# Places of matmul operands in SBUF: odd and even multiples of 64 bytes for the weight buffers and the FFN inputs of a two-layer decoder trunk

## Chip, core and metric

The kernel runs on one core of one Trainium2 chip. The metric is the device time of one launch in microseconds; lower is better. Before the change the median of three runs is 2210.63 us (2208.31 to 2213.5).

## What is computed

A decoder trunk of two layers works on x of 512 tokens by 1024 features, all in float32. Cut to what matters:

```python
def swiglu(h, w_gate, w_up, w_down):
    return (jax.nn.silu(h @ w_gate) * (h @ w_up)) @ w_down

for i in range(DEPTH):                       # DEPTH = 2
    x = x + 0.5 * swiglu(rmsnorm(x, g[0]), ...)   # D_FF = 2816
    h = rmsnorm(x, g[1])
    x = x + (attn_mixer(h, ...) if i % 2 == 0 else mamba2_mixer(h, ...))
    x = x + 0.5 * swiglu(rmsnorm(x, g[2]), ...)
return rmsnorm(x, final_norm)
```

So there are four FFNs (`swiglu`), one attention mixer and one state-space mixer (SSM), in the order FFN 0, attention, FFN 1, FFN 2, SSM, FFN 3.

## The kernel before

Everything is kept transposed: features on the 128 partitions, tokens along the free dimension. Every float32 product is made of three TensorE matmuls on a split of both operands, `a = ah + al`: `mm3` (lines 121 to 125) issues weights `whi` with moving `xh` (line 123), `whi` with `xl` (line 124) and `wlo` with `xh` (line 125). Each matmul loads its own 128 x 128 weights first, so in the profile each PE MATMUL has a PEld LDWEIGHTS with the same operands. The program gives the moving operand as the last input of a matmul and the weights as the first; the profile prints the moving operand first (`bs<-xh,whi`: output `bs`, moving `xh`, weights `whi`).

- **Weights.** A weight tile comes from HBM into `raw` (two buffers, SyncE's queue). `split` (line 92) makes `whi` by a rounding copy on ScalarE (line 98) and `wlo` by a subtraction on VectorE (line 99). `split_dma` (line 104) makes `whi` and a negated copy on ScalarE (lines 110, 111) and adds `raw` by a DMA of GpSimd's queue (line 112). `whi` and `wlo` have three buffers each, used in turn, in one pool (line 46). Each buffer is 4096 bytes in a partition. `values` (line 373) takes its value weights from the same buffers.
- **FFN inputs.** `open_x` (line 144) opens a pool at the upper end of SBUF before each stage. For an FFN `xh` and `xl` are 32768 bytes each: for every one of 4 feature blocks 8 pieces of 256 tokens, seven of which are the operands of a Strassen scheme, so that a gate and up block takes 7 products instead of 8. For the attention and the SSM they are 16384 bytes each and a filler tile of 64 bytes follows (line 158). `edge` (line 50) takes the last 32 bytes.
- **One FFN** (`ffn`, line 1096) has two halves. In each, 11 calls of `gate_up` (line 1176) make 7 products x 4 feature blocks x 3 = 84 matmuls of 256 columns each (output `bs`), and then the down projection makes 8 x 11 x 3 = 264 matmuls of 512 columns (output `bm`, moving `ah`, `al`). The first block of each FFN (the first two of FFN 0) has no Strassen scheme: `gate_up_direct` (line 1139), 2 x 8 x 3 = 48 matmuls of 512 columns. The last output tile of FFN 3 is made in two halves of 256 columns by `last` (line 1263).
- **The rest.** The projections of the attention and the SSM are `mm3` of 512 columns with moving `xh`, `xl`, the output projections have moving `qh`, `ql` and `yh`, `yl`.

The order of the instructions on each engine is set by a scheduler when the program is built, with time estimates of its own; the tile pools give each tile its place in SBUF, from the lower end or from the upper end (`side="right"`). The places of the built program, in bytes from the start of a partition: `whi` 33664, 37760, 41856, `wlo` 45952, 50048, 54144, `ah` 78720, `al` 101248; `xh` 163776 and `xl` 196544 in all four FFNs; `xh` 196480 and `xl` 212864 in the attention and the SSM. Divided by 64 the FFNs' `xh` and `xl` give odd numbers, all the others even ones. Every slice that a matmul of these tiles takes starts a multiple of 128 bytes into its tile, except half of those of `values`, so the tile's place tells odd or even.

Of the kernel before, what the change touches and what calls it, by code (L numbers as in the profile page):

```python
# [14 lines left out]
F32 = mybir.dt.float32  # L15
F32R = mybir.dt.float32r
# [5 lines left out]
P = 128  # L22
# [7 lines left out]
FFN_NORMS = (0, 2, 3, 5)  # L30
# [10 lines left out]
class Trunk:  # L41
    def __init__(self, ctx, tc, aps):
        self.ctx, self.tc, self.nc, self.aps = ctx, tc, tc.nc, aps
        nc = self.nc
        self.cst = ctx.enter_context(tc.tile_pool(name="cst", bufs=1))
        self.wp = ctx.enter_context(tc.tile_pool(name="wp", bufs=3))
        self.rawp = ctx.enter_context(tc.tile_pool(name="rawp", bufs=2))
        self.one = ctx.enter_context(tc.tile_pool(name="one", bufs=1))

        edge = ctx.enter_context(tc.tile_pool(name="edge", bufs=1, side="right"))  # L50
        edge.tile([P, 8], F32, name="edge")
        self.xT = self.cst.tile([P, ND, T], F32, name="xT")
        self.xpool = None
        self.gains = self.cst.tile([P, 7, ND], F32, name="gains")
        nc.sync.dma_start(out=self.gains, in_=aps["gains"])
        self.epsc = self.cst.tile([P, 1], F32, name="epsc")
        nc.vector.memset(self.epsc, EPS)
        self.onesD = self.cst.tile([P, P], F32, name="onesD")
        nc.vector.memset(self.onesD, 1.0 / D)
        self.n = 0  # L60
        self.ahead = None
        nc.scalar.preload_act_table_set("natural_log_exp_and_others")
# [25 lines left out]
    def row(self, tag):  # L88
        self.n += 1
        return self.one.tile([P, T], F32, tag=tag, name=f"{tag}_{self.n}")  # L90

    def split(self, raw, n, lo_engine=None):

        nc = self.nc
        self.n += 1
        hi = self.wp.tile([P, 8, P], F32R, tag="whi", name=f"whi_{self.n}")
        lo = self.wp.tile([P, 8, P], F32R, tag="wlo", name=f"wlo_{self.n}")
        nc.scalar.copy(out=hi[:, :n], in_=raw)  # L98
        (lo_engine or nc.vector).tensor_tensor(  # L99
            out=lo[:, :n], in0=raw, in1=hi[:, :n].bitcast(F32), op=ALU.subtract  # L100
        )
        return hi, lo

    def split_dma(self, raw, n):

        nc = self.nc
        self.n += 1
        hi = self.wp.tile([P, 8, P], F32R, tag="whi", name=f"whi_{self.n}")
        lo = self.wp.tile([P, 8, P], F32R, tag="wlo", name=f"wlo_{self.n}")
        nc.scalar.copy(out=hi[:, :n], in_=raw)  # L110
        nc.scalar.activation(out=lo[:, :n], in_=raw, func=AF.Copy, scale=-1.0)  # L111
        nc.gpsimd.dma_start(out=lo[:, :n], in_=raw, accum_op=ALU.add)  # L112
        return hi, lo
# [30 lines left out]
    def open_x(self):  # L144

        self.close_x()
        self.r = None
        if self.which == 6:
            return
        self.n += 1  # L150
        self.strassen = self.which in FFN_NORMS
        self.xpool = self.tc.tile_pool(name=f"x{self.n}", bufs=1, side="right", reuse_waits="tile")
        pool = self.xpool.__enter__()
        shape = [P, 4, 8, 256] if self.strassen else [P, ND, T]
        self.xh = pool.tile(shape, F32R, name=f"xh_{self.n}")
        self.xl = pool.tile(shape, F32R, name=f"xl_{self.n}")
        if not self.strassen:
            pool.tile([P, 16], F32, name=f"xe_{self.n}")

    def close_x(self):  # L160
# [212 lines left out]
    def values(self, rc):  # L373

        nc, aps, A = self.nc, self.aps, self.A
        gate = A.tile([P, NB, 24], F32, name="gate")
        banks = [self.bank(t) for t in "ttom"]
        for c in range(4):
            raw = self.load(aps["wv"][:, 2 * c : 2 * c + 2], [P, 2, 408])
            self.n += 1  # L380
            hi = self.wp.tile([P, 2, 408], F32R, tag="whi", name=f"whi_{self.n}")
            lo = self.wp.tile([P, 2, 408], F32R, tag="wlo", name=f"wlo_{self.n}")
            nc.scalar.copy(out=hi, in_=raw)
            nc.gpsimd.tensor_tensor(out=lo, in0=raw, in1=hi.bitcast(F32), op=ALU.subtract)
            for j in range(2):
                k = 2 * c + j
                for t in range(NB):
                    ts = slice(t * P, t * P + P)
                    self.mm3(
                        banks[t][:, 0:408], self.xh[:, k, ts], self.xl[:, k, ts], hi[:, j], lo[:, j], k == 0, k == ND - 1  # L390
                    )
        for t in range(NB):
            b = banks[t]
            src = b[:, 0:384].rearrange("p (a g d) -> p a g d", a=3, g=2)
            dst = [v[:, t].rearrange("p a (h d) -> p a h d", h=3)[:, :, 0:3:2] for v in (self.vh, self.vl)]
            nc.scalar.activation(out=dst[0], in_=src, func=AF.Copy, scale=rc[:, t : t + 1])
            for g in range(2):
                nc.vector.scalar_tensor_tensor(
                    out=dst[1][:, :, g],
                    in0=src[:, :, g],  # L400
                    scalar=rc[:, t : t + 1],
                    in1=dst[0][:, :, g].bitcast(F32),
                    op0=ALU.mult,
                    op1=ALU.subtract,
                )
            nc.vector.tensor_scalar(
                out=gate[:, t], in0=b[:, 384:408], scalar1=rc[:, t : t + 1], scalar2=None, op0=ALU.mult
            )
        nc.scalar.activation(out=gate, in_=gate, func=AF.Exp, scale=-1.0)
        nc.vector.tensor_scalar(out=gate, in0=gate, scalar1=1.0, scalar2=None, op0=ALU.add)  # L410
        nc.vector.reciprocal(out=gate, in_=gate)
        self.gate = gate.rearrange("p t (g j r) -> p t g j r", g=2, j=4)
# [985 lines left out]
```

## Time and profile before

| | |
|---|---|
| median of three runs | 2210.63 us (2208.31 to 2213.5) |
| the profiled execution | 2213.22 us, of which the span of its instructions is 2211.4 us |
| PE (matmul) busy | 2139.6 us, 97% of the span, 13488 matmuls |
| PEld (weight loads) busy | 1919.7 us, 87% |
| VectorE, ScalarE, GpSimd busy | 75%, 52%, 36% |
| granted TensorE clock, mean | 0.987 of full speed |
| chain that ended last | PE 85%, VectorE 8%, ScalarE 3%, issue 2%, DMA 2% |

The profiled execution is one launch on the chip. The time of a launch is the span plus what lies around it, here 2213.22 - 2211.4 = 1.8 us. A matmul's end in the profile is modelled (matmuls overlap in the array), so its duration tells little; the time from one matmul's start to the next one's start is what a stream of them costs. The chain is followed back from the last instruction, at each step to what released it.

### The profile page before, as it was taken

Reading aid. Unit: us, or ns where it says so; the run is one execution under the profiler, and the core shown is the slowest. Engines: PE = TensorE matmul, PEld = TensorE weight load, DVE = VectorE, ACT = ScalarE, POOL = GpSimd, SP = SyncE. Lnnn points to the kernel's source line nnn. Section 1 sums busy time; section 2 is a strip of 40 time slices with the busy share of each in tenths; the row PEclk is TensorE's granted clock in tenths of the full one; section 3 lists DMA queues with packets and bytes.
Section 4 is the critical chain, followed back from the end, with each engine's and each line's share of the span. In section 5 each row is a group of like instructions: output and inputs, shape, how many; then the busy total and the mean of one; then the engine's idle time right before and its main releaser. Section 6 shows DMA issues by size and latency. Waiting matters only on the chain.

```text
span 2211.4 us, 34462 instructions
## 1 busy us (share of the span) xinstructions
PE 2139.6 (97%) x13488; PEld 1919.7 (87%) x13488; DVE 1659.7 (75%) x2495; ACT 1157.1 (52%) x1813; POOL 805.4 (36%) x602
## 2 busy tenths in 40 slices
PE   8999999988999999999999999999999998999997
PEld 6999997877887998998998997788888877998996
DVE  6966975586788976987985985677667668975974
ACT  7533544455566533545542544677667666543543
POOL 1613621532013623622632630244444435623630
PEclk9999999979999999999999999999999999999999
DMA  3222325416302322322332324656565652232332
GB/s 134 96 100 102 115 99 155 128 49 154 77 1 67 115 98 103 108 102 94 109 104 97 115 93 127 153 144 152 125 155 144 162 143 61 102 106 101 109 104 78
DMA packets 48450, 242.05 MB, mean 109 GB/s; under 512 B 6624, under 2 KB 9696, under 8 KB 31136
## 3 DMA queue, kind: packets, MB, share of 16 engines
q1 hardware_dynamic: 36048, 195.28, 25.7%
q0 software_dynamic: 12240, 44.57, 10.7%
q8 instruction: 106, 1.74, 0.3%
q14 instruction: 56, 0.46, 0.1%
HBM read 193.04 MB, written 2.23 MB: 88 GB/s over the span
## 4 chain that ended last, share of the span: by engine, by line
PE 85%; DVE 8%; ACT 3%; issue 2%; DMA 2%; POOL 0%; SPq 0%; DVEq 0%; ACTq 0%; POOLq 0%
PE bm L123 13%; PE bm L125 13%; PE bm L124 13%; PE bs L123 13%; PE bs L125 12%; PE bs L124 12%; DMA wlo<-raw 1%; PE bt L541 1%; DVE wlo L99 1%; DVE xl L249 1%; PE bs L492 1%; PE bo L556 1%; PE bs L487 1%; PE bo L553 1%; PE bs L493 0%
## 5 line engine op out<-in xcount | busy, mean ns | idle before, releaser
L123 PE MATMUL bs<-xh,whi 128*128 128x256 f32 (+1 forms) x2404 | 680.0, 286 | 7.6 <-ACT xh L248 3.6
L124 PE MATMUL bs<-xl,whi 128*128 128x256 f32 (+1 forms) x2404 | 679.8, 285 | 5.7 <-DVE xl L249 5.7
L125 PE MATMUL bs<-xh,wlo 128*128 128x256 f32 (+1 forms) x2404 | 669.2, 285 | 2.0 <-DVE wlo L99 1.9
L98 ACT CAST whi<-raw 128x1024 fp32r<-128x1024 f32 (+3 forms) x312 | 257.0, 827 | 403.5 <-PE bm L124 188.1
L123 PEld LDWEIGHTS bs<-xh,whi 128*128 128x128 f32 x2404 | 452.1, 188 | 17.6 <-ACT whi L98 5.8
L124 PEld LDWEIGHTS bs<-xl,whi 128*128 128x128 f32 x2404 | 452.0, 188 | 12.6 <-DVE xl L249 7.6
L125 PEld LDWEIGHTS bs<-xh,wlo 128*128 128x128 f32 x2404 | 446.7, 188 | 7.9 <-DVE wlo L99 2.8
L99 DVE TENSOR_TENSOR wlo<-raw,whi 128x1024 fp32r<-128x1024 f32 (+3 forms) x304 | 332.2, 1093 | 91.3 <-ACT whi L98 89.8
L1173 POOL TENSOR_TENSOR sa<-raw 128x512 f32<-128x512 f32 x82 | 113.2, 1381 | 654.7 <-DMA raw<-wgu 297.8
L125 PE MATMUL bm<-ah,wlo 128*128 128x512 f32 (+1 forms) x715 | 275.9, 386 | 0.0
L124 PE MATMUL bm<-al,whi 128*128 128x512 f32 (+1 forms) x715 | 275.8, 386 | 0.0
L123 PE MATMUL bm<-ah,whi 128*128 128x512 f32 (+1 forms) x715 | 274.8, 386 | 0.0
L112 POOL DMA_DIRECT2D wlo<-raw x85 | 73.7, 867 | 449.5 <-ACT wlo L111 443.9
L123 PE MATMUL bm<-xh,whi 128*128 128x512 f32 x488 | 194.2, 398 | 5.8 <-DVE t L858 3.5
L125 PE MATMUL bm<-xh,wlo 128*128 128x512 f32 x488 | 192.8, 395 | 4.2 <-DMA wlo<-raw 4.1
L124 PE MATMUL bm<-xl,whi 128*128 128x512 f32 x488 | 192.4, 395 | 0.0
L1173 POOL TENSOR_TENSOR sa<-sa,raw 128x512 f32<-128x512 f32 x82 | 166.6, 2031 | 5.6
L125 PEld LDWEIGHTS bm<-ah,wlo 128*128 128x128 f32 x715 | 134.3, 188 | 27.2
L124 PEld LDWEIGHTS bm<-al,whi 128*128 128x128 f32 x715 | 134.3, 188 | 26.8
L123 PEld LDWEIGHTS bm<-ah,whi 128*128 128x128 f32 x715 | 134.3, 188 | 26.8
L99 DVE TENSOR_TENSOR wlo<-sb,whi 128x1024 fp32r<-128x1024 f32 x83 | 150.8, 1817 | 0.0
L1218 DVE TENSOR_TENSOR gu<-gu,bs 128x512 f32<-128x512 f32 (+1 forms) x249 | 147.4, 592 | 2.7
(400 smaller groups left out, 4168.9 us busy)
## 6 DMA issues: line engine op xcount, KB each, us to landing
raw<-wgu SPq DMA_DIRECT2D x88, 1024.0 KB
raw<-wdn SPq DMA_DIRECT2D x64, 704.0 KB
wlo<-raw POOLq DMA_DIRECT2D x85, 512.0 KB, 4.7
raw<-m_win SPq DMA_DIRECT2D x24, 1024.0 KB
raw<-m_wout SPq DMA_DIRECT2D x8, 1024.0 KB
raw<-wqk SPq DMA_DIRECT2D x6, 1024.0 KB
raw<-cw SPq DMA_DIRECT2D x4, 1024.0 KB
raw<-wo SPq DMA_DIRECT2D x4, 1024.0 KB
```

The source lines that it names most:

```text
L98: nc.scalar.copy(out=hi[:, :n], in_=raw)
L99: (lo_engine or nc.vector).tensor_tensor(out=lo[:, :n], in0=raw, in1=hi[:, :n].bitcast(F32), op=ALU.subtract)
L112: nc.gpsimd.dma_start(out=lo[:, :n], in_=raw, accum_op=ALU.add)
L123: nc.tensor.matmul(out, wh, xh, start=start, stop=False)
L124: nc.tensor.matmul(out, wh, xl, start=False, stop=False)
L125: nc.tensor.matmul(out, wl, xh, start=False, stop=stop)
L249: nc.vector.tensor_tensor(out=lo, in0=src, in1=hi.bitcast(F32), op=ALU.subtract)
L487: nc.tensor.matmul(s[j], q_hi, k_hi, start=True, stop=False)
L492: nc.tensor.matmul(s[j], q_hi, k_lo, start=False, stop=False)
L541: nc.tensor.transpose(t[:, at : at + P], p[:, j, k0 : k0 + P], self.idf)
L1173: engine.tensor_tensor(out=out, in0=x, in1=y, op=op)
L1218: nc.vector.tensor_tensor(out=out, in0=x, in1=y, op=ALU.add)
```

## The change

It changes where tiles stand in SBUF and nothing else. The instructions, their order on each engine and their semaphore waits are the same in both built programs.

```diff
-        self.wp = ctx.enter_context(tc.tile_pool(name="wp", bufs=3))
+        self.wph = ctx.enter_context(tc.tile_pool(name="wph", bufs=3))
+        apart = ctx.enter_context(tc.tile_pool(name="apart", bufs=1))
+        apart.tile([P, 16], F32, name="apart")
+        self.wpl = ctx.enter_context(tc.tile_pool(name="wpl", bufs=3))
+        apart2 = ctx.enter_context(tc.tile_pool(name="apart2", bufs=1))
+        apart2.tile([P, 16], F32, name="apart2")
...
+    def weight_tiles(self):
+        tiles = (
+            pool.tile([P, 8 * P + 16], F32R, tag=tag, name=f"{tag}_{self.n}")
+            for pool, tag in ((self.wph, "whi"), (self.wpl, "wlo"))
+        )
+        return [t[:, : 8 * P].rearrange("p (k m) -> p k m", m=P) for t in tiles]
...
-        hi = self.wp.tile([P, 8, P], F32R, tag="whi", name=f"whi_{self.n}")
-        lo = self.wp.tile([P, 8, P], F32R, tag="wlo", name=f"wlo_{self.n}")
+        hi, lo = self.weight_tiles()
...
+        form = FFN_NORMS.index(self.which) if self.strassen else 1
         self.xh = pool.tile(shape, F32R, name=f"xh_{self.n}")
+        if form > 1:
+            pool.tile([P, 16], F32, name=f"xm_{self.n}")
         self.xl = pool.tile(shape, F32R, name=f"xl_{self.n}")
-        if not self.strassen:
+        if form in (1, 2):
             pool.tile([P, 16], F32, name=f"xe_{self.n}")
```

`split` and `split_dma` take their tiles from `weight_tiles`, `values` from `wph` and `wpl`. A weight buffer grows by 64 bytes, so the middle one of the three stands at an odd multiple of 64. The places after the change:

| tile | before | after |
|---|---|---|
| `whi`, three buffers | 33664 even, 37760 even, 41856 even | 33664 even, 37824 odd, 41984 even |
| `wlo`, three buffers | 45952 even, 50048 even, 54144 even | 46208 even, 50368 odd, 54528 even |
| `xh`, `xl` of FFN 0 | 163776 odd, 196544 odd | 163776 odd, 196544 odd |
| `xh`, `xl` of FFN 1 | 163776 odd, 196544 odd | 163712 even, 196480 even |
| `xh`, `xl` of FFN 2 | 163776 odd, 196544 odd | 163648 odd, 196480 even |
| `xh`, `xl` of FFN 3 | 163776 odd, 196544 odd | 163712 even, 196544 odd |
| `xh`, `xl` of attention, SSM | 196480 even, 212864 even | the same |
| `ah`, `al` | 78720 even, 101248 even | 79232 even, 101760 even |

The other tiles from the lower end stand 512 bytes higher, and so keep odd or even.

## Rows read from the trace of the kernel before

**Rows 1.** The page: busy time of the engines (us, share of span, instructions), then the chain.

```profile
PE 2139.6 (97%) x13488; PEld 1919.7 (87%) x13488; DVE 1659.7 (75%) x2495; ACT 1157.1 (52%) x1813; POOL 805.4 (36%) x602
...
PE 85%; DVE 8%; ACT 3%; issue 2%; DMA 2%; POOL 0%; SPq 0%; DVEq 0%; ACTq 0%; POOLq 0%
```

**Rows 2.** Groups by line and shape: count, busy us, mean ns, idle before, releasers.

```profile
L123 PE MATMUL bs<-xh,whi 128*128 128x256 f32 x2324 | 647.3, 281 | 2.6 <-ACT whi L98 1.1 <-DVE al L249 0.7 <-DVE gu L1218 0.3
...
L123 PE MATMUL bm<-ah,whi 128*128 128x512 f32 x693 | 268.4, 389 | 0.0
L123 PE MATMUL bm<-xh,whi 128*128 128x512 f32 x488 | 194.2, 398 | 5.8 <-DVE t L858 3.5 <-DVE xT L1234 1.6 <-DVE z L858 0.7
...
L123 PE MATMUL bm<-yh,whi 128*128 128x512 f32 x128 | 51.0, 402 | 0.0
...
L123 PE MATMUL bm<-qh,whi 128*128 128x512 f32 x64 | 26.4, 412 | 0.7 <-ACT qh L248 0.7
```

**Rows 3.** Busy us (instructions) of PE by stretch, granted clock, DMA share, GB/s.

```profile
196.20:304.90 108.70, 108.70 (x925) 1.00 0.29 101
136.40:196.10 59.70, 59.70 (x265) 1.00 0.31 108
2189.35:2194.60 5.25, 5.25 (x46) 1.00 0.00 0
1030.90:1041.80 10.90, 10.90 (x49) 1.00 0.28 96
```

**Rows 4.** Timeline of PE, start and duration in us: FFN 0, gate and up, second half.

```profile
196.18 0.28 PE L123 MATMUL bs<-xh,whi 128*128 128x256 f32 x1
...
305.00 0.40 PE L123 MATMUL bm<-ah,whi 128*128 128x512 f32 x1
```

**Rows 5.** The same view: FFN 3, last output tile, 256 columns.

```profile
2189.29 0.28 PE L123 MATMUL bm<-ah,whi 128*128 128x256 f32 x1
...
2194.69 0.38 PE L1284 MATMUL bs<-acc,onesD 128*128 128x256 f32 x1
```

**Rows 6.** The same view: FFN 0, first down projection, 512 columns.

```profile
136.31 0.39 PE L123 MATMUL bm<-ah,whi 128*128 128x512 f32 x1
...
195.95 0.39 PE L125 MATMUL bm<-ah,wlo 128*128 128x512 f32 x1
```

**Rows 7.** The same view: FFN 2, the block without Strassen, 512 columns.

```profile
1030.82 0.40 PE L123 MATMUL bs<-xh,whi 128*128 128x512 f32 x1
...
1041.83 0.59 PE L138 MATMUL bm<-acc,onesD 128*128 128x512 f32 x1
```

**Rows 8.** Groups by line and shape, ScalarE, whole span.

```profile
L248 ACT CAST xh<-t 128x512 fp32r<-128x512 f32 x32 | 19.6, 614 | 8.5 <-DVE t L207 5.7 <-DVE t L211 2.7
...
L1077 ACT CAST yh<-gy 128x512 fp32r<-128x512 f32 x16 | 9.7, 622 | 5.6 <-DVE gy L1072 5.6
```

**Rows 9.** Groups by line and shape, VectorE, from 1035 to 1060 us.

```profile
L249 DVE TENSOR_TENSOR al<-bs,ah 128x512 fp32r<-128x512 f32 x1 | 0.7, 684 | 0.0
L249 DVE TENSOR_TENSOR xl<-s,xh 128x512 fp32r<-128x512 f32 x1 | 0.7, 679 | 0.0
```

More of the change, by code (lines that the diff above doesn't have):

```diff
@@ L107, in split_dma @@
         self.n += 1
-        hi = self.wp.tile([P, 8, P], F32R, tag="whi", name=f"whi_{self.n}")
-        lo = self.wp.tile([P, 8, P], F32R, tag="wlo", name=f"wlo_{self.n}")
+        hi, lo = self.weight_tiles()
         nc.scalar.copy(out=hi[:, :n], in_=raw)
@@ L380, in values @@
             self.n += 1
-            hi = self.wp.tile([P, 2, 408], F32R, tag="whi", name=f"whi_{self.n}")
-            lo = self.wp.tile([P, 2, 408], F32R, tag="wlo", name=f"wlo_{self.n}")
+            hi = self.wph.tile([P, 2, 408], F32R, tag="whi", name=f"whi_{self.n}")
+            lo = self.wpl.tile([P, 2, 408], F32R, tag="wlo", name=f"wlo_{self.n}")
             nc.scalar.copy(out=hi, in_=raw)
```

## The prediction

> **What bounds the kernel now.** I read the page first. TensorE is busy for 2139.6 us of the 2211.4 us span, and 85% of the chain that ended last is PE [rows 1]; no other engine is near. So what a matmul costs is what the kernel costs, and the groups by line and shape come next, for where the matmuls are: 3 x 2324 with 256 columns in the gate and up blocks, with almost no idle time before them, 3 x 693 with 512 columns in the down projections with none, and some 3 x 700 of 512 columns in the two mixers [rows 2]. The durations in these rows are no price, because successive matmuls overlap in the array: the mean of 281 ns times 6972 would be 1959 us. The price is the time from start to start. I take it from the timeline, in stretches in which PE is busy without a gap and at full clock: in all four windows the busy time equals the window and the clock is 1.00 [rows 3].
>
> Odd and even below mean the multiple of 64 bytes at which an operand stands. While a matmul streams its moving operand, the weights of the next one are loaded, so each step has two reads of SBUF side by side. In the kernel before all weights are even; only the moving operand differs. The stretches give:
>
> - 256 columns, moving odd, weights even (gate and up): from 196.18 to 305.00 us there are 11 x 84 = 924 matmuls [rows 4], 108.82 us / 924 = **117.8 ns**.
> - 256 columns, moving even, weights even (the last output tile): 33 matmuls of its first half and 12 of the second, 45 from 2189.29 to 2194.69 us [rows 5], 5.40 us / 45 = **120.0 ns**.
> - 512 columns, moving even, weights even (down projection): 263 steps from 136.31 to 195.95 us [rows 6], 59.64 us / 263 = **226.8 ns**.
> - 512 columns, moving odd, weights even (block without Strassen): 48 from 1030.82 to 1041.83 us [rows 7], 11.01 us / 48 = **229.4 ns**.
>
> The same shape thus has two prices by place: with 256 columns the unequal pair is 2.2 ns cheaper than the equal one, with 512 columns it is 2.6 ns dearer. The kernel before has the cheap kind at nearly all its matmuls.
>
> **What the change does, part by part.** It adds and removes no instruction, wait or DMA, and no order changes on any engine. I count, in the program's order, each matmul's moving operand against the weights that the next one loads. One in three buffers becomes odd, so about a third of the weight loads do.
>
> (a) Gate and up, 256 columns, 6972 matmuls. FFN 0 keeps odd `xh` and `xl` and meets odd weights a third of the time: 563 of 1680 become equal. FFN 1 has both even: two thirds, 1183 of 1764. FFN 2 has `xh` odd (two of three matmuls) and `xl` even: 399 + 388 = 787. FFN 3 is the reverse: 785 + 196 = 981. Together 3514 matmuls go from unequal to equal, and 3514 x 2.2 ns = **+7.7 us**. That equal-odd costs what equal-even costs is assumed; no row before has odd weights. Its bounds are taken from the rows for 256 columns: nothing (the place of the moving operand alone counts, see the second rival), or the 2.2 ns. I take the 2.2 ns, because in the rows what differs is the pair.
>
> (b) 512 columns with even moving operand: 691 steps of the down projections, 116 and 45 of the attention's input and output projections, 367 and 132 of the SSM's, 1351 in all, get an odd weight tile next and go from equal to unequal: 1351 x 2.6 ns = **+3.5 us**. The other way, 75 of the 240 in the blocks without Strassen go from unequal to equal: -0.2 us. Here the bounds are wide. The 229.4 ns come from stages in which two outputs take turns, at the start of an FFN, so the 2.6 ns may belong to the stage and not to the place. The lower bound is then what 256 columns show, -2.2 ns, or -2.8 us over the net 1276; the upper one is +2.6 ns, +3.3 us. I take the upper, because its row has the same column count.
>
> (c) ScalarE, VectorE, GpSimd and DMA. Their operands move too, and I cost that at nothing: ScalarE writes the odd `xh` in 614 ns and the even `yh` in 622 ns, same shape [rows 8]; VectorE writes the odd `xl` in 679 ns and the even `al` in 684 ns [rows 9]. If a split slowed all the same, the cover is the idle quarter of VectorE and half of ScalarE [rows 1].
>
> (d) What reaches the end. Gate, up and down stretches of the FFNs run without a gap, so (a) and 691 x 2.6 = 1.8 us of (b) arrive whole. The mixers' 660 steps are worth 1.7 us, in stages where 15% of the chain is not PE and PE waits for VectorE and DMA; I let half of it arrive, and take 0.9 us off.
>
> The sum: 7.7 + 3.5 - 0.2 - 0.9 = **+10.1 us**. The profiled execution would go from 2213.22 to 2223.3 us. It lies 2.6 us above the median of the runs, so for the time I add to the median: 2210.63 + 10.1 = **2220.7 us**, 0.46% slower.
>
> **The rivals.**
>
> 1. *With 512 columns unequal is cheaper too.* The price of 229.4 ns would be the stage's, not the place's. For it: the outputs take turns there. Against it: all four FFNs have such a block, and the rows of one show the price over 48 steps. It gives 7.7 - 2.8 = +4.9 us, 2215.5 us.
>
> 2. *Only the moving operand's place counts.* Then odd weights do nothing, and the 256-column matmuls whose moving operand becomes even pay: all 1764 of FFN 1, the 588 with `xl` of FFN 2, the 1176 with `xh` of FFN 3, 3528 x 2.2 = +7.8 us; 96 steps without Strassen gain 0.2. FFN 0 and the down projections stay as they are. No row speaks against it. It gives 2218.2 us.
>
> 3. *Places do not matter.* The 120.0 ns would come from the last output tile's own stage, the 229.4 ns from the first block's. The four prices are one stage each, which is what speaks for it; that a step's price differs by 2 ns at the same shape, with no idle time and full clock, speaks against it. It gives no change, 2210.6 us. The Trainium skill has this rule: in "TensorE: Matmul & The Clock Gate", Part 2, step-by-step, it says that TensorE has two independent read ports, so loading the next weights takes no read bandwidth from the running matmul. By that rule the sum is 0; the rows speak against it so far as the two prices of one shape belong to the place.
>
> 4. *An odd weight tile makes its step cheaper by itself, whatever moves beside it.* This is the case on the other side. Its place is the 2330 weight loads of gate and up and the 1351 of the rest that become odd. Taken at the largest difference that a place shows, 2.6 ns, that is 3681 x 2.6 = -9.6 us; the 2356 gate and up steps left with even moving and even weights still pay 2.2 ns, +5.2 us. It gives -4.4 us, 2206.2 us. It decides the sign from 5.2 / 3681 = 1.4 ns per odd load upwards, and is measurable only at 2.6 ns. Room for it exists: between equal pairs of 256 and 512 columns a column costs (226.8 - 120.0) / 256 = 0.417 ns, so 120.0 ns hold 120.0 - 106.8 = 13.2 ns that are not streaming. Against it: no row shows such a load.
>
> That the change does not do what it says can be left out: the places of the built program are as the table of the change gives them.
>
> **How the numbers follow.** A difference of 0.2% (4.4 us) is about what a measurement of this kernel can tell from no change. Chances: the forecast 0.55, rival 1 0.12 (it lies at the edge of 0.2%, half counted as slower), rival 2 0.12, rival 3 0.11, rival 4 0.10. Slower: 0.55 + 0.06 + 0.12 = 0.73. Same: 0.06 + 0.11 = 0.17. Faster: 0.10. The range holds the forecast and rivals 1 and 2, 0.79: from 2212.5 us (rival 1's 2215.5 less about 3 us, as the runs shown lie up to 2.9 us from their median) to 2226 us (the forecast with (d) undone, 2221.6, and with as much for the runs and for mixed places of `xh` and `xl`, which no row shows).
>
> **What would show it right or wrong.** In the profile after, a stretch of 924 gate and up matmuls without a gap should take, by mean price per step: FFN 0 118.5 ns (a third equal), FFN 1 119.3, FFN 2 118.8, FFN 3 119.0; a down projection 227.6 ns instead of 226.8. The idle rows of PE and the waits should stay. If FFN 0 stays at 117.8 and FFN 1 is at 120.0, rival 2 is right; if the down projections fall below 226.8, rival 1 or 4; if all four FFNs stay at 117.8, rival 3. A change in waits of more than a few us, or a stretch at a lower clock, would make the sum wrong in a way that none of these cases holds.

## The result and the profile after

| | before | after |
|---|---|---|
| median, four runs of each | 2211.84 us (2208.31 to 2213.5) | 2228.39 us (2223.65 to 2230.75) |
| profiled execution, its span | 2213.22 us, 2211.4 us | 2228.97 us, 2227.2 us |
| granted TensorE clock, mean | 0.987 | 0.984 |

The ratio is 1.0075 [1.0059, 1.0091]: 16.6 us slower. The forecast had the sign, but said 2220.7 us and a range up to 2226. The page first, the rows that answer to [rows 1]:

```profile
PE 2157.3 (97%) x13488; PEld 1922.3 (86%) x13488; DVE 1659.0 (74%) x2495; ACT 1157.2 (52%) x1813; POOL 803.8 (36%) x602
...
PE 85%; DVE 6%; ACT 3%; DMA 3%; issue 2%; POOL 1%; SPq 0%; DVEq 0%; ACTq 0%; POOLq 0%
```

The picture is the same, and PE is still 85% of the chain. PE is busy for 17.7 us more (2157.3 - 2139.6), the span is 15.8 us longer, and the other engines work as long as before (VectorE 1659.0 us against 1659.7, ScalarE 1157.2 against 1157.1). So the time went into the steps of TensorE. Which ones, the groups by line and shape begin to tell (`mm3` is now lines 134 to 136):

```profile
L134 PE MATMUL bs<-xh,whi 128*128 128x256 f32 x2324 | 648.9, 281 | 3.2 <-DVE al L264 1.5 <-ACT whi L110 0.9 <-ACT xh L263 0.4
...
L134 PE MATMUL bm<-ah,whi 128*128 128x512 f32 x693 | 271.4, 393 | 0.0
L134 PE MATMUL bm<-xh,whi 128*128 128x512 f32 x488 | 195.9, 402 | 5.8 <-DVE t L873 3.5 <-DVE xT L1249 1.6 <-DVE z L873 0.7
```

Against [rows 2] the 256-column group rose by only 1.6 us, and the two of 512 columns by 3.0 and 1.7; the waits before the 512-column rows are unchanged. The forecast had put most of the loss at 256 columns. For the prices I take starts again, in stretches without a gap. The windows of PE (us, busy and instructions, granted clock, DMA share, GB/s) for the second gate and up half of FFN 0 up to its first longer step, the first down projection of FFN 0, the attention and the SSM:

```profile
195.50:273.30 77.80, 77.80 (x675) 1.00 0.31 106
...
134.40:195.30 60.90, 60.90 (x265) 1.00 0.32 106
365.79:686.72 320.93, 297.63 (x1817) 0.95 0.35 88
1380.33:1858.85 478.52, 466.62 (x2285) 0.99 0.59 145
```

In the first two, busy time equals the window and the clock is 1.00, as in [rows 3]: at the same level of the clock the steps themselves changed. The timeline of PE (start, duration, instruction), in the order of time:

```profile
64.81 0.28 PE L134 MATMUL bs<-xh,whi 128*128 128x256 f32 x1
...
66.25 0.28 PE L134 MATMUL bs<-xh,whi 128*128 128x256 f32 x1
...
67.61 0.28 PE L134 MATMUL bs<-xh,whi 128*128 128x256 f32 x1
...
134.26 0.40 PE L134 MATMUL bm<-ah,whi 128*128 128x512 f32 x1
...
149.58 0.40 PE L134 MATMUL bm<-ah,whi 128*128 128x512 f32 x1
...
153.79 0.39 PE L134 MATMUL bm<-ah,whi 128*128 128x512 f32 x1
...
157.21 0.40 PE L134 MATMUL bm<-ah,whi 128*128 128x512 f32 x1
...
161.39 0.40 PE L134 MATMUL bm<-ah,whi 128*128 128x512 f32 x1
...
195.39 0.28 PE L134 MATMUL bs<-xh,whi 128*128 128x256 f32 x1
...
273.41 0.39 PE L136 MATMUL bs<-xh,wlo 128*128 128x256 f32 x1
...
302.89 0.40 PE L134 MATMUL bm<-ah,whi 128*128 128x512 f32 x1
...
863.67 0.28 PE L134 MATMUL bs<-xh,whi 128*128 128x256 f32 x1
...
973.06 0.40 PE L134 MATMUL bm<-ah,whi 128*128 128x512 f32 x1
...
1208.62 0.28 PE L134 MATMUL bs<-xh,whi 128*128 128x256 f32 x1
...
1318.66 0.39 PE L134 MATMUL bm<-ah,whi 128*128 128x512 f32 x1
...
2042.22 0.28 PE L134 MATMUL bs<-xh,whi 128*128 128x256 f32 x1
...
2151.53 0.40 PE L134 MATMUL bm<-ah,whi 128*128 128x512 f32 x1
```

Which buffer a matmul's weights stand in comes from the program's order, laid beside the trace. Three things are to be seen.

- **Gate and up.** FFN 0: 674 steps in 78.02 us, 115.8 ns, cheaper than the 117.8 ns of [rows 4]; the whole half, with five longer steps of 183 to 227 ns, takes 107.50 us, 116.3 ns. FFN 1, 2 and 3: 924 steps in 109.39, 110.04 and 109.31 us, 118.4, 119.1 and 118.3 ns.
- **FFN 0 by buffer.** 12 steps with the middle buffer take 1.44 us (64.81 to 66.25), 120 ns, and the next 12 with the first buffer 1.36 us (to 67.61), 113.3 ns. No row before has that price over a whole stage.
- **Down.** 264 steps take 61.13 us (134.26 to 195.39), 231.6 ns, where [rows 6] had 226.8. By buffer: 18 steps with the middle one 4.21 us (from 149.58), 233.9 ns; 15 with the first 3.42 us, 228.0 ns; 18 with the third 4.18 us, 232.2 ns. The third buffer is even, as the moving operand is, and was counted as unchanged.

Step by step along the program, the profiled execution after differs from the one before by: gate and up +0.9 us, down +9.25 us (2079 steps, 4.45 ns each), attention, SSM and what lies around them +6.1 us (the SSM +4.4, from 474.1 us to the 478.5 of its window), blocks without Strassen -0.5 us. Together +15.8 us. The SSM's window in the profile of before:

```profile
1371.41:1845.51 474.10, 460.94 (x2284) 0.99 0.59 146
```

### The profile page after: what moved, and what is told of

It is laid out like the page before. It is cut to its first block, busy times and chain, and to the rows that moved or that the text cites. A ratio compares the mean times of both kernels' runs of the same rounds, so it can differ in the third digit from the quotient of the medians.

```text
span 2227.2 us, 34462 instructions
## 1 busy us (share of the span) xinstructions
PE 2157.3 (97%) x13488; PEld 1922.3 (86%) x13488; DVE 1659.0 (74%) x2495; ACT 1157.2 (52%) x1813; POOL 803.8 (36%) x602
## 4 chain that ended last, share of the span: by engine, by line
PE 85%; DVE 6%; ACT 3%; DMA 3%; issue 2%; POOL 1%; SPq 0%; DVEq 0%; ACTq 0%; POOLq 0%
PE bm L134 13%; PE bm L135 13%; PE bm L136 13%; PE bs L136 13%; PE bs L135 13%; PE bs L134 13%; DMA wlo<-raw 1%; PE bt L556 1%; DVE wlo L111 1%; DVE xl L264 1%; PE bs L507 1%; PE bo L571 1%; PE bs L502 1%; PE bo L568 1%; PE bs L508 0%
```

## The experiments

The forecast went by odd and even, that is by places modulo 128. But the place moved in two ways at once: the middle weight buffer went 64 bytes on, the third 128 bytes on. Modulo 256, the places were 128 for all weights, for `ah` and `al` and for the mixers' operands, and 192 for the FFNs' `xh` and `xl`. They are now 128, 192 and 0 for the three weight buffers, 128 for `ah` and `al`, and for `xh`/`xl` 192/192, 128/128, 64/128 and 128/192 in the four FFNs.

**Theory M** (its name in the expectations): a step's price goes by the distance of the moving operand from the next weights, modulo 256 bytes. At 512 columns distance 0 is the cheapest. At 256 columns distance 0 costs 120.0 ns, and at other distances a stream of steps sits in one of two steady patterns, 113.3 or 117.8 ns a step; which one is set by what ran before. e2, e3, e6 and e7 correct parts of it. **Rivals:** the forecast's odd and even pairs; the place of one operand by itself; the distance from `whi` to `wlo`.

The ratios below are to the kernel before, run on the same chip; where none stands the time is that of a single run.

### One half of the change at a time

**e1**: the weights as in the change, the FFNs' operands as before:

```diff
-        form = FFN_NORMS.index(self.which) if self.strassen else 1
+        form = 0 if self.strassen else 1
```

> The weight buffers as in the change, xh and xl of all four FFNs as before (odd, odd). Theory M (places count modulo 256 bytes, and a run of matmuls settles into one of several steady patterns): FFN 1 to 3 behave as FFN 0 of the changed kernel, gate and up at 115.7 ns a step instead of 117.8, 6972 x -2.1 = -14.6 us; the steps of 512 columns keep the whole loss of the changed kernel, +9.3 us in the down projections and +6.1 us in the mixers. Sum about +1 us, 2210 to 2215 us. Rival (the low price of FFN 0 belongs to the first FFN, not to the places): gate and up of FFN 1 to 3 stay at 117.8 or rise to 118.5, sum +12 to +18 us. Theory of the prediction (odd and even as a pair, fixed prices): 118.5 in all four FFNs, +5 us there, +2.5 us at 512 columns.

Measured: 2219.61 us (2217.66 to 2223.73), ratio 1.0040 [1.0025, 1.0056]. Timeline of PE, FFN 2's second gate and up half; then, in the window view, FFN 3 soon after the SSM:

```profile
1202.56 0.28 PE L134 MATMUL bs<-xh,whi 128*128 128x256 f32 x1
...
1309.48 0.40 PE L134 MATMUL bm<-ah,whi 128*128 128x512 f32 x1
```

```profile
1875.60:1879.00 3.40, 3.40 (x21) 0.62 0.00 0
```

The 924 steps take 106.92 us, 115.7 ns: the odd buffer at 120.0, the two others at 113.7 and 113.3. Gate and up gain 4.3 us over the whole program, the first blocks 3.1 us, and the 512-column work loses what it loses in the change (down +9.25, mixers and the rest +5.5). So the weights alone make all of the loss at 512 columns, and at 256 columns they are a gain. The whole came out dearer than Theory M expected because FFN 3 did not take part: its second half took 118.4 ns a step, and its first one lost 2.8 us more, part of it in the stretch of the window above, where the granted clock is 0.62 on average (for most of it the lower level, 1.2 GHz) after PE had stood idle for about 2 us. In the profile of before the clock falls earlier, 0.74 from 1862 to 1868 us, in FFN 3's block without Strassen; so the gain of the first blocks, 2.9 us of it in FFN 3, may be the other side of this loss and not an effect of places. Why FFN 3 kept the dear pattern at the same places as FFN 1 and 2 is open.

**e2**: the weights as before, the FFNs' operands as in the change:

```diff
+        form = FFN_NORMS.index(self.which) if self.strassen else 1
         self.xh = pool.tile(shape, F32R, name=f"xh_{self.n}")
+        if form > 1:
+            pool.tile([P, 16], F32, name=f"xm_{self.n}")
         self.xl = pool.tile(shape, F32R, name=f"xl_{self.n}")
-        if not self.strassen:
+        if form in (1, 2):
```

> The weight buffers as before (all even, all at 128 modulo 256), xh and xl as in the change. Theory of the prediction: FFN 0 117.8 ns, FFN 1 120.0, FFN 2 (xl even) 118.5, FFN 3 (xh even) 119.3; +7.9 us, about 2219 us. Theory M: FFN 0 117.8, FFN 1 120.0 (equal places), but FFN 2 and FFN 3, where xh and xl stand at different distances from the weights, settle at values of their own that are not these means. Both: steps of 512 columns stay at 226.8 ns.

Measured: 2218.91 us (2218.08 to 2220.47), ratio 1.0038 [1.0023, 1.0053]. Timeline of PE: FFN 0's first gate and up half, its second, and FFN 1's second:

```profile
56.87 0.28 PE L123 MATMUL bs<-xh,whi 128*128 128x256 f32 x1
...
122.94 0.28 PE L123 MATMUL bs<-xh,whi 128*128 128x256 f32 x1
...
123.67 0.28 PE L123 MATMUL bs<-xh,whi 128*128 128x256 f32 x1
...
132.85 0.39 PE L123 MATMUL bm<-ah,whi 128*128 128x512 f32 x1
...
192.71 0.28 PE L123 MATMUL bs<-xh,whi 128*128 128x256 f32 x1
...
301.54 0.40 PE L123 MATMUL bm<-ah,whi 128*128 128x512 f32 x1
...
858.51 0.28 PE L123 MATMUL bs<-xh,whi 128*128 128x256 f32 x1
...
969.38 0.40 PE L123 MATMUL bm<-ah,whi 128*128 128x512 f32 x1
```

FFN 1, both operands at distance 0: 924 steps in 110.87 us, 120.0 ns, as the even pair of [rows 5]. FFN 0 has nothing moved at all, and shows both patterns: 583 steps in 66.07 us are **113.3 ns** each, and 924 in 108.83 us **117.8 ns**, with the same places, instructions and granted clock (1.00). Between them lie a longer step of 0.39 us, 81 more steps at 113.3 ns (123.67 to 132.85 us) and the down projection: the longer step did not end the cheap pattern. So price is not a function of places alone.

In FFN 2 and FFN 3 the second halves took 118.8 and 119.1 ns. The forecast's fixed prices give 118.5 and 119.3, so they nearly hold here, and Theory M, which expected values of their own, missed. Gate and up lose 3.7, 1.9 and 2.3 us in FFN 1, 2 and 3, where counting at 2.2 ns gives 3.9, 1.3 and 2.6; FFN 0 gains 3.2 us by its pattern. At 512 columns nothing changed (down +0.05 us). The two halves of the change, 7.7 and 7.0 us over their 2211.92 us, make 14.7 of the 16.6 us, which the intervals do not tell from the whole.

### The distances themselves

**e3**, one table for both shapes: the weights as before, `xh`/`xl` at distances 64, 0, -64, -128 in FFN 0 to 3, `ah`/`al` at 0, 64, 128, -64.

```diff
-        if not self.strassen:
-            pool.tile([P, 16], F32, name=f"xe_{self.n}")
+        if form:
+            pool.tile([P, 16 * form], F32, name=f"xe_{self.n}")
...
+            if 2 * li + fi:
+                ap.tile([P, 16 * (2 * li + fi)], F32, name=f"ae{li}{fi}")
```

> All weights as before. xh and xl stand 64, 0, -64 and -128 bytes from the weights modulo 256 in FFN 0, 1, 2, 3; ah and al 0, 64, 128 and -64 bytes. Theory of the prediction (odd or even only): gate and up 117.8, 120.0, 117.8, 120.0 ns; down 226.8, 229.4, 226.8, 229.4 ns. Theory M: distance 128 differs from distance 0, and -64 may differ from 64: gate and up 117.8, 120.0, then two other values between 113 and 120; down 226.8, then about 233, 231, 233.

Measured: 2226.76 us. Timeline of PE: FFN 1's first down half, FFN 2's block without Strassen, first down half and second gate and up half, FFN 3's second gate and up half:

```profile
803.56 0.40 PE L123 MATMUL bm<-ah,whi 128*128 128x512 f32 x1
...
865.16 0.29 PE L123 MATMUL bs<-xh,whi 128*128 128x256 f32 x1
...
1037.64 0.39 PE L123 MATMUL bs<-xh,whi 128*128 128x512 f32 x1
...
1048.84 0.59 PE L138 MATMUL bm<-acc,onesD 128*128 128x512 f32 x1
...
1149.11 0.40 PE L123 MATMUL bm<-ah,whi 128*128 128x512 f32 x1
...
1210.45 0.28 PE L123 MATMUL bs<-xh,whi 128*128 128x256 f32 x1
...
1319.27 0.40 PE L123 MATMUL bm<-ah,whi 128*128 128x512 f32 x1
...
2039.44 0.28 PE L123 MATMUL bs<-xh,whi 128*128 128x256 f32 x1
...
2149.08 0.39 PE L123 MATMUL bm<-ah,whi 128*128 128x512 f32 x1
```

| distance | 512 columns (264 steps) | 256 columns (924 steps) |
|---|---|---|
| 0 | 226.8 ns | 120.0 ns |
| 64 | 61.60 us, 233.3 ns | 117.8 ns |
| -64 | 233.3 ns | 108.82 us, 117.8 ns |
| 128 | 61.34 us, 232.4 ns | 109.64 us, 118.7 ns |

This is the run that settles the 512 columns: an even pair at distance 128 is dear too (232.4 ns), so the pairs of odd and even fall, and a whole stage at one distance has one price. The loss of down in the change follows: a third of the steps each at 226.8, 233.3 and 232.4 ns make 230.8, where FFN 0's first half took 231.6. At 256 columns the 118.7 ns at distance 128 are neither of the two patterns. The block without Strassen of FFN 2, here at distance -64, takes 11.20 us for its 48 steps, 233.3 ns, where the same block at 64 took 229.4 [rows 7].

**e6**, a finer table: distances of 32 and 96 bytes to either side, for `xh`/`xl` 32, -32, -96, 96 and for `ah`/`al` 32, 96, -32, -96 (the expectation has the last two the other way round; the filler tiles of 224 bytes in FFN 2 and 160 in FFN 3 give -32 and -96):

```diff
+            pool.tile([P, (8, 24, 40, 56)[form]], F32, name=f"xe_{self.n}")
...
+            ap.tile([P, (8, 24, 56, 40)[2 * li + fi]], F32, name=f"ae{li}{fi}")
```

> All weights as before. xh and xl stand 32, -32, -96 and 96 bytes from the weights modulo 256 in FFN 0, 1, 2, 3; ah and al 32, 96, -96 and -32 bytes. Theory M with blocks of 64 bytes, in which only the block counts: a distance of 32 is half equal and half one block on, so gate and up at 118 to 120 ns and down between 226.8 and 233.3 ns; 96 lies between 64 and 128, gate and up 117.8 to 118.7, down 232.3 to 233.3. Rival (finer grain: each distance has a price of its own): some distance leaves the bands, perhaps towards the 113.3 ns or below 226.8 ns.

Measured: 2227.85 us. Timeline of PE, FFN 0's first down half (distance 32), 264 steps in 61.59 us:

```profile
133.60 0.39 PE L123 MATMUL bm<-ah,whi 128*128 128x512 f32 x1
...
195.19 0.28 PE L123 MATMUL bs<-xh,whi 128*128 128x256 f32 x1
```

All eight down halves rose by 1.7 to 2.0 us over their 264 (or 231) steps, to 233.3 ns and FFN 3 to 234.3. A distance of 32 already costs the whole 6.5 ns; I had thought it might cost part. At 256 columns the second halves gave 117.8 ns (distance 32), 118.3 (-32), 118.7 (-96) and 120.0 (96), so the two patterns of Theory M are not the only prices there, and 96 costs what 0 does. The grain is 32 bytes or finer, and of the distances tried only 0 is cheap at 512 columns.

**e8**, all tiles moved together by 64 bytes modulo 256:

```diff
+        self.cst.tile([P, 16], F32, name="low")
...
-        edge.tile([P, 8], F32, name="edge")
+        edge.tile([P, 56], F32, name="edge")
```

> The kernel before with every tile 64 bytes further modulo 256: weights, ah, al and the mixers' operands now stand at odd, the FFNs' xh and xl at even multiples of 64; all distances are as before. Theory M (only the distance of weights and moving operand counts): 117.8 ns and 226.8 ns as before, 2205 to 2214 us. Rival (the moving operand's own place counts): gate and up 120.0, down 229.4 ns, +15 and +6 us, 2231 us. Rival (an odd weight tile is cheaper by itself): all steps 2 ns or more cheaper, below 2190 us.

Measured: 2211.17 us (2206.97 to 2217.45), ratio 1.0001 [0.9989, 1.0014]. The same stretch as [rows 4], in the timeline of PE:

```profile
195.35 0.28 PE L124 MATMUL bs<-xh,whi 128*128 128x256 f32 x1
...
304.18 0.40 PE L124 MATMUL bm<-ah,whi 128*128 128x512 f32 x1
```

924 steps in 108.83 us, 117.8 ns, and the down projections at 226.8. All weights are now odd and all distances are what they were: neither the moving operand's place nor the weights' place counts by itself. Weights moved alone (e1) and moving operand moved alone (e3) both cost at 512 columns; moved together they do not.

**e4**, the `wlo` buffers alone, 256 bytes further from `whi`, with two pools and their filler tiles as in the change:

```diff
+        apart.tile([P, 64], F32, name="apart")
```

> Everything as before, but the three wlo buffers stand 256 bytes further up, as the first of them does in the changed kernel. Theory M: nothing changes, gate and up 117.8, down 226.8 ns, within 0.3% of the kernel before. Rival (FFN 0 of the changed kernel is cheaper because whi and wlo no longer stand at the same place modulo 512): gate and up fall towards 113.3 ns in all FFNs, -14 to -31 us.

Measured: 2211.82 us, 117.8 and 226.8 ns in the stretches without a gap, as before. So 256 bytes more between the two weight tiles change nothing, and a distance of 256 is as good as none.

### Bringing the stream into the cheap pattern

**e7**: in e1 a passage through an equal pair seemed to leave the stream at 113.3 ns. Each gate and up block has 7 products; the smallest change that makes one such passage is to put the 4 weight tiles of `a22`, the last product (12 of 84 steps), 64 bytes into their buffers, at distance 0 from `xh` and `xl`:

```diff
-    def split(self, raw, n, lo_engine=None):
+    def split(self, raw, n, lo_engine=None, at=0):
...
+        hi = self.wp.tile([P, 8 * P], F32R, tag="whi", name=f"whi_{self.n}")
+        lo = self.wp.tile([P, 8 * P], F32R, tag="wlo", name=f"wlo_{self.n}")
+        hi, lo = (a[:, at : at + n * P].rearrange("p (k m) -> p k m", m=P) for a in (hi, lo))
...
-        w = self.split(a22, 4)
+        w = self.split(a22, 4, at=16)
```

> The kernel before, but the weights of the fourth product (a22, 12 of the 84 matmuls of a gate and up block) stand 64 bytes into their buffers, at the same place modulo 256 as xh and xl. Down projections and mixers keep their places, 226.8 ns. Theory M1 (leaving an equal pair puts the stream into the 113.3 ns pattern): gate and up (72 x 113.4 + 12 x 119.9) / 84 = 114.3 ns, 6972 x -3.5 = -24 us, about 2188 us. Theory M2 (an equal pair only hands the pattern on, and a stall of the stream sets it): each FFN half is at 114.3 or at 118.1 ns, by what the stall before it left; between -24 and +2 us.

Measured: **2204.38 us** (2201.55 to 2206.07), ratio 0.9971 [0.9959, 0.9984]: faster than both kernels. Timeline of PE in FFN 0:

```profile
204.35 0.28 PE L124 MATMUL bs<-xh,whi 128*128 128x256 f32 x1
...
207.07 0.28 PE L124 MATMUL bs<-xh,whi 128*128 128x256 f32 x1
...
209.79 0.28 PE L124 MATMUL bs<-xh,whi 128*128 128x256 f32 x1
...
211.23 0.28 PE L124 MATMUL bs<-xh,whi 128*128 128x256 f32 x1
```

Twice 24 steps in 2.72 us, 113.3 ns, then the 12 of `a22` in 1.44 us, 120 ns. These 12 begin with the first matmul of `a22` and end with its last; if the next matmul's weights set the price, they would begin and end one step earlier. So by the recorded starts a matmul's own weights count, where Theory M says the next ones; within a buffer the two have the same place, so the distances above stand.

Gate and up gain 10.8 us of the profiled execution, the down projections change by nothing; M1's 2188 us is missed, M2's range holds. About 60% of the 72 main steps of a block run at 113.3 ns. Where no step of 135 ns or more stood among the 12 equal steps or the 12 behind them, a stream at 113.3 ns came out at 113.3 in 25 of 29 cases, and one at 117.8 came out at 113.3 in 20 of 30. With such a longer step among the 12 behind, the cheap pattern was lost in 16 of 19.

**e9**, the same with `a22` split and multiplied first in each block, to see whether the place in the block matters:

```diff
-        return a22, [self.split(a, 8) for a in (raw[:, 0], sa, sb)]
+        return self.split(a22, 4, at=16), [self.split(a, 8) for a in (raw[:, 0], sa, sb)]
...
-        for a in todo:
+        for a in [(p4, a22, 0, 6)] + todo:
```

> As the run with a22's weights 64 bytes into their buffers, but each gate and up block makes the product of a22 first, so that the short wait at a block's first matmuls comes before the 12 equal steps and not behind them. The sums are the same, only their order changes. Theory M: in that run the 113.3 ns pattern was left after such waits and taken up again behind equal steps; with this order it holds for most of each block, gate and up at 114.5 to 115.5 ns, 2190 to 2198 us. Rival (the order of the blocks does not matter for the pattern): about 2204 us as in that run, or slower if the new order makes TensorE wait for the weights.

Measured: 2211.93 us (2206.36 to 2214.47), ratio 1.0004 [0.9992, 1.0016], a miss. Gate and up gain 5.3 us in the profiled execution, half of e7's gain, and the rest of the program loses 4.5: the first blocks are 2.0 us longer, and of the mixers, which the edit does not touch, the SSM is 6.8 us longer and the attention 3.7 us shorter. The steps of gate and up below 135 ns have nearly the mean of e7 (115.6 and 115.8 ns), so the new order did not hold the cheap pattern longer; the longer steps (94, in e7 70) cost 6.4 us more than there.

**e10**, `a22` at another distance in each FFN, -64, -128, 32 and -32 from its operands, and last in the block again:

```diff
-        w = self.split(a22, 4)
+        w = self.split(a22, 4, at=(32, 48, 8, 24)[2 * li + fi])
```

> As the run with a22's weights shifted in their buffers, but shifted by another amount in each FFN, so that xh and xl stand -64, -128, 32 and -32 bytes from those weights (modulo 256) in FFN 0, 1, 2, 3 instead of 0; all other weights stay at distance 64. Theory M: a block at another distance than its neighbours can move the stream from the 117.8 ns to the 113.3 ns pattern, whatever the distance; some 10 of each FFN's 21 blocks are then at 113.3 ns and each FFN's mean lies between 114 and 117 ns. Rival (only equal places do that): the FFNs stay at 117.8 ns, apart from the 12 of 84 steps at their own price (118 to 120 ns).

Measured: 2206.49 us, beside 2210.07 us for the kernel before, a single run of each. Timeline of PE: FFN 0 (distance -64), and FFN 2's second gate and up half (distance 32):

```profile
194.06 0.28 PE L124 MATMUL bs<-xh,whi 128*128 128x256 f32 x1
...
242.10 0.28 PE L125 MATMUL bs<-xl,whi 128*128 128x256 f32 x1
...
1196.09 0.28 PE L124 MATMUL bs<-xh,whi 128*128 128x256 f32 x1
...
1304.92 0.39 PE L124 MATMUL bm<-ah,whi 128*128 128x512 f32 x1
```

In FFN 0, 421 steps in 48.04 us are 114.1 ns each, `a22` among them; in FFN 2 924 steps in 108.83 us are 117.8 ns, as if nothing had been moved, and the second halves of FFN 1 and 3 take 117.9 and 117.8 ns. So of the distances tried for `a22` only 0 and -64 take the stream to the cheap pattern. (The two times, one run each, do not tell the kernels apart; the steps do.) The natural next kernel, **e11**, puts `a22` at -64 in all four FFNs, where its own steps are cheap as well:

```diff
-        w = self.split(a22, 4)
+        w = self.split(a22, 4, at=32)
```

> a22's weights 128 bytes into their buffers in all four FFNs, so that xh and xl stand -64 bytes from them and 64 bytes from all other weights, as in FFN 0 of the run before. Theory M: as that FFN 0, gate and up at 114.7 ns a step with the waits between the patterns, about -3.2 us per FFN, -13 us, 2198 us. Rival (FFN 0 fell into the 113.3 ns pattern by itself): FFN 1 to 3 stay at 117.8 ns, 2207 us.

Measured: 2203.25 us (2201.02 to 2205.44), ratio 0.9972 [0.9959, 0.9985]. Each FFN has such a stretch of 421 steps at 114.1 ns, so FFN 0 was no exception, and gate and up gain 8.5 us, less than expected: only about half of the main steps are at 113.3 ns. In FFN 0, 1 and 3 the stretch ends at one longer step of 0.37 us. The time is not told apart from e7.

**e12**, the kernel before once more, unchanged, to see how much of a pattern comes of itself:

> The kernel before, unchanged, one more look. Theory M: gate and up at 117.8 ns in most stretches; if the pattern is set by stalls, a stretch at 113.3 ns may show in another execution of the same program, most likely behind a wait. Rival (places alone set it): the same stretches at the same price in every execution.

Measured: 2210.87 us. All four second gate and up halves took 108.83 us and all down halves what they took before, to 0.01 us. In gate and up only the first halves of FFN 0 and FFN 3 differ, by 0.6 and 0.4 us. The 113.3 ns appear in short stretches: in FFN 3, some 165 steps here and 82 in the profile of before. So a stretch without a gap repeated itself from one execution to the next, and the differences above are far over that. The stages with waits did not repeat: the attention is 2.1 us shorter here than in the profile of before, the SSM 2.6 us longer, with nothing changed.

## Why the prediction was wrong, point by point

- **What bounds the kernel** was right: the loss is in TensorE's steps, at full clock, without new waits (the idle rows of the 512-column groups are unchanged), and the prices by start to start are the view that shows it. The count took each matmul's moving operand against the next one's weights; e7 points to its own ones, which shifts the count by one step at either end of a buffer and changes the sums little.
- **The rule by odd and even** failed. It was read from four rows that had only distances 64 and 0. Four rows fit the pair of parities and the distance modulo 256 alike; the change has distances that only the second tells apart.
- **Step (a), +7.7 us; measured +0.9.** Its assumption that an equal pair of odd places costs what an equal even pair costs held: 120.0 ns in FFN 0's middle buffer. With the operands alone moved (e2) the 2.2 ns came out too. What failed is that an unequal step costs 117.8 ns whatever ran before it. In FFN 0 the passages through the odd buffer left the two other buffers' steps at 113.6 instead of 117.8, and the FFN gained 3.3 us where 563 x 2.2 = 1.2 us of loss were counted. Of the 3.3 us, 2.0 lie in its first half, and e2, with FFN 0's places as before, gained 3.2 us there: that part shows the pattern and need not come from the buffer. The means by FFN were 116.3, 118.4, 119.1 and 118.3 ns, forecast 118.5, 119.3, 118.8 and 119.0.
- **Step (b), +3.5 us, of it 1.8 in down; measured +9.25 in down and most of +6.1 in the mixers.** This is the step that makes the miss. First, the price: the middle buffer costs 6.5 ns at distance -64 (e3: 233.3 - 226.8), not 2.6. The 229.4 ns of [rows 7], taken as the upper bound, were no bound: they are a price at distance 64, and the same block at -64 costs 233.3 ns (e3). Why it is cheaper at 64 than a down projection at 64 (233.3) is open; its two outputs take turns, and its moving operand comes in two pieces of 256 columns (`gate_up_direct`). Second, the count: the third buffer, even and so left out, costs 5.6 ns (232.4 - 226.8) at distance 128. With both, 512-column steps of the down projections rise by 4.45 ns on average; in the mixers those of 215 to 260 ns rise from 228.6 to 231.4 ns, some 1950 steps x 2.8 = 5.5 us. Every run with the mixers' distances as before has 228.6 or 228.7 there, the two with other distances (the change and e1) 231.4. The prices of e3 would make some 8 us, so the mixers pay less than a down projection does; why is open.
- **The 75 steps without Strassen, -0.2 us:** -0.5 us measured, of the right sign; too small to say more.
- **Step (c), nothing from the other engines,** held: VectorE's and ScalarE's busy times are as before to 0.7 us.
- **Step (d), half of the mixers hidden,** is not settled. The SSM's window is 4.4 us longer, its PE busy for 5.7 us more (466.62 against 460.94); attention and SSM together take 5.5 us longer, in e1 4.9 us, which looks as if nothing were hidden. But in the ten experiments in which the mixers' distances are those of before (all but e1), the two stages together lie between 3.9 us under and 4.1 us over the profile of before.
- **Rival 1** falls: unequal is dearer at 512 columns in the change and in e3 (233.3 against 226.8 ns). **Rival 2 and rival 4**, one operand's own place, fall with e8 (ratio 1.0001 with all weights odd). **Rival 3**, no effect of places, falls with e3: 61.60 against 59.87 us for the same 264 steps. The rule of the Trainium skill named there ("TensorE: Matmul & The Clock Gate", Part 2, step-by-step: two independent read ports, so loading weights takes no read bandwidth) gives a sum of 0. Here places alone move a step of 512 columns by 6.5 ns (e3), and the measurement decides. Whether it is the ports, the runs do not say.

By the prices of e3 the down part of step (b) comes out within a microsecond: 2079 x (0 + 6.5 + 5.6) / 3 = 8.4 us against 9.25. Step (a) does not come out from prices alone: the pattern depends on what ran before, and e1 and e2 show gate and up at -4.3 and +4.7 us for the two halves and +0.9 for both. That the forecast had the sign and two thirds of the size, 10.1 of the profile's 15.8 us, is in part luck: it was 6.8 us too high in (a) and some 12 us too low at 512 columns, and the two errors offset each other.

**Left open.** What in the chip makes the two patterns, and why distances 0 and -64 lead into the cheap one and the other distances that were tried do not. A kernel with the middle buffer 128 bytes on and no odd place was not run; distance 128 is in e3.

## What to carry to other kernels

Where matmuls stream back to back with a fresh weight tile each, look at the starts of a stretch without a gap and compare the places of moving operand and weights modulo 256 bytes. In this kernel, 512-column steps were cheapest at distance 0 and 256-column ones at 64 (117.8 or 113.3 ns, 120.0 at 0), so one padding for both shapes loses at one of them; pad the buffers of one stage, not a pool that all stages share. And a price read from a single stage is a price of that stage: four rows that differ in two things at once fit more than one rule, and a bound taken from one of them is no bound.

## What the runs showed that was not expected

- Same instructions, places and clock, two steady prices: 113.3 and 117.8 ns a step of 256 columns (e2, FFN 0). The cheap one lasted for 583 steps, and for 81 more behind one longer step.
- At 512 columns a distance of 32 bytes costs as much as one of 64: 233.3 against 226.8 ns (e6, e3).
- Moving 12 of 84 weight loads by 64 bytes, with nothing else changed, makes the kernel 0.29% faster (e7, ratio 0.9971 [0.9959, 0.9984]); by 128 bytes 0.28% (e11).
